# Layer 0's scale and shift dots of the second norm, placed beside the attention

## The chip, the cores and the metric

The kernel runs on one core of one Trainium2 chip. The metric is the device time of one execution, in microseconds (us). Engines are named as the profile names them: PE (TensorE) multiplies matrices, PEld loads its weights, DVE (VectorE) and ACT (ScalarE) work on whole tiles, POOL (GpSimd) and SP (SyncE) here issue transfers.

## The reference

Two layers of a decoder trunk on 512 tokens of width 1024, all in float32. Cut to what matters here:

```python
mod = (c_act @ w_ada + b_ada)[:, None, :]            # c_act = silu(c), one vector of 1024
sh1, sc1, g1, sh2, sc2, g2 = jnp.split(mod, 6, axis=-1)
h = rmsnorm(x, norm1_w) * (1 + sc1) + sh1
u = h @ w_in                                         # pool, conv, q, k, v, gate logits
...                                                  # pooling, short convolution, attention
merged = (gates[:, :, 0] * (y_pool @ p_pool)
          + gates[:, :, 1] * (y_conv @ p_conv)
          + gates[:, :, 2] * (y_attn @ p_attn))
x = x + g1 * (merged @ w_out)
h2 = rmsnorm(x, norm2_w) * (1 + sc2) + sh2
x = x + g2 * ((silu(h2 @ w_gate) * (h2 @ w_up)) @ w_down)
```

The modulation `mod` does not depend on `x`. Its six parts have 1024 numbers each; every one is a dot product of `c_act` with a column of `w_ada`.

## The kernel before, in words

**Matrix work.** Activations lie with features on the 128 partitions and the 512 tokens along the row, as eight tiles. Every product is made of three matmuls (`mm3`): both operands are split into a high and a low part, and high x high, high x low, low x high are summed. The low part of an activation is made on ACT and DVE (`split_from`, L671 to L680: a copy L675, a subtraction L676). Weights come in chunks of eight 128x128 blocks (512 KB) through a ring of three `raw` buffers; ACT writes the high part `whi`, DVE subtracts for `wlo` (`split_w`, L397 to L404). Chunks of the gate columns are split otherwise (`split_by_transfer`, L416 to L424): ACT writes `wlo` as minus the high part, and a transfer that POOL issues adds the weights from memory (L423). `next_w` keeps up to `ahead_now` chunks loaded ahead.

**The dots.** Of one part of `mod`, 128 numbers are one DVE instruction over a tile of 128x1024 (`ada_dot`, L477 to L480), so a part has eight dots. Each needs its own 512 KB load on SP's queue (L513). `ada_tasks` (L530) makes a list of tasks with a cost: 1.2 for a dot, 0.2 for a part's closing arithmetic. With `early` the loads go to the `raw` ring and stand one dot ahead; the first task is a load alone. Without it they go to the six spare tiles `w4`, which the attention uses too.

**What sets the order.** Side work stands in a list `bulk`. After every 2048 columns of `mm3`, that is, 12 full matmuls, there is a tick. It advances the running pieces of the attention (`fibers`) and then calls `run_bulk` with `bulk_rate`:

```python
credit[0] = min(credit[0] + amount, 4.0)
while bulk and credit[0] >= 0:
    cost, fn = bulk.popleft()
    credit[0] -= cost
    fn()
```

Credit goes on growing, up to 4, while the list is empty. `flush_bulk` runs what is left at once; `drain` ticks until no fiber is left. The framework's planner then orders each engine's instructions; those that are pinned (matmuls, weight splits on DVE, dots) keep program order among themselves on their engine.

**The stages around the change.** Once keys and values are there, three gates are computed, then convolution and pooling, then a fourth gate (`ready`). A loop over eight pairs `j` (L1212) then computes two gates each (two ticks a gate, those made ahead excepted) and the gated sum of pooling and convolution (one tick; L1209, L1226, into `m01`). The third gates and the attention's output follow in the order `GATE2`: six gates, attention steps 0 and 1, gates 6 and 7, attention steps 2 to 7. An attention step (L1244 to L1252) is 12 matmuls, the gated product L1209, the addition L1251 and the split into `merged[j]`. The attention itself runs in the ticks from before the fourth gate up to step 0, where `drain` ends it: scores, softmax on DVE and ACT (L796 to L817), transposes on PE (L161), products with the values. Behind it `tail` (L1261) makes the output projection, eight columns of 24 matmuls over `merged[0]` to `merged[7]`, adds it to `x` with `g1`, and prepares the second norm; the dots of G2 run beside it.

In layer 0, SC2's eight dots go through the `raw` ring beside the attention; the rate is 0 up to the third pair and 0.25 from there. G1's eight dots and, behind them, SH2's eight run at rate 1.5 from attention step 0 on. In layer 1 only G1 (rate 1.3) is left at that place, since SC2 and SH2 were made earlier; its list is empty beside the attention.

Of the kernel before, what the change touches and what calls it, by code (L numbers as in the profile page):

```python
# [63 lines left out]
SH1, SC1, G1, SH2, SC2, G2 = range(6)  # L64
# [19 lines left out]
def hybrid_trunk(ctx, tc, xT, ws, ada, cols, pool_w, qk_w, crow, pos, con, out):  # L84
# [22 lines left out]
    def ps_mm():  # L107
        return psum.tile([P, S], F32, tag="mm", name=nm("mm"), bufs=4)
# [16 lines left out]
    bulk = deque()  # L125
    bulk_rate, credit = [0.0], [0.0]
# [8 lines left out]
    def flush_bulk():  # L135
        while bulk:
            bulk.popleft()[1]()
# [12 lines left out]
    def drain():  # L150
        while fibers:
            tick()
# [10 lines left out]
    def mm3(o, lhs, rhs, start, stop, main=True, **more):  # L163
        matmul(o, lhs[0], rhs[0], start=start, stop=False, **more)
        matmul(o, lhs[0], rhs[1], start=False, stop=False, **more)
        matmul(o, lhs[1], rhs[0], start=False, stop=stop, **more)
        if main:
            clock[0] += o.shape[-1]
            if clock[0] >= TICK:
                clock[0] -= TICK  # L170
                tick()
# [105 lines left out]
    class GateUp:  # L277
# [9 lines left out]
        def load(self, sub):  # L287
            if sub < 2:
                return self.pair[sub].first()
            if sub < 6:  # L290
                return self.pair[sub % 2].sums(sub // 2 - 1)
            raw = rawt()
            fetch(raw, self.l, self.pair[0].blocks(1, 1) + self.pair[1].blocks(1, 1))
            return split_w(raw, C_BLOCKS)
# [159 lines left out]
    def next_w(ahead=None):  # L454
        ahead = ahead_now[0] if ahead is None else ahead
        while at[0] < len(items) and len(loaded) <= ahead:
            loaded.append(load_w())
        return loaded.popleft()

    def wblk(w, b):  # L460
        return w[0][:, b, :], w[1][:, b, :]
# [49 lines left out]
    def ada_load(l, part, j, early, kept):  # L511
        aw = wp.tile([P, D], F32, tag="raw", name=nm("raw"), bufs=RAW) if early else w4([P, D])
        nc.sync.dma_start(aw, ada[l, part, j])  # L513
        kept.append(aw)

    def ada_step(l, part, j, kept):
        aw = kept.pop(0)
        with tc.issue_after(dots_after[0].ins) if dots_after[0] is not None else nullcontext():
            ins = ada_dot(aw, l, part, j)
        pin(ins)  # L520

    def ada_end(l, part):
        m = mod[l][:, part]
        V.tensor_add(m, m, colt[:, l, C_ADA + part * KT:C_ADA + (part + 1) * KT])
        if part in (SC1, SC2):
            fold_scale(l, 0 if part == SC1 else 1, 0, KT)
        if part == G1:
            V.tensor_scalar(m, m, 0.5, None, op0=ALU.mult)

    def ada_tasks(l, parts, early=False):  # L530
        every = [(part, j) for part in parts for j in range(KT)]
        kept, out = [], []
        load = lambda n: ada_load(l, *every[n], early, kept)

        def step(n):
            if early and n + 1 < len(every):
                load(n + 1)
            if not early:
                load(n)
            ada_step(l, *every[n], kept)  # L540

        if early:
            out.append((1.2, lambda: load(0)))
        for n, (part, j) in enumerate(every):
            out.append((1.2, lambda n=n: step(n)))
            if j == KT - 1:
                out.append((0.2, lambda part=part: ada_end(l, part)))
        return out
# [122 lines left out]
    def split_from(src, scale=None):  # L671

        hi, lo = bigt(), bigt()
        if scale is None:
            A.activation(hi, src, AF.Copy)  # L675
            last_split[0] = V.tensor_sub(lo, src, f32(hi))  # L676
        else:
            A.activation(hi, src, AF.Copy, scale=scale)
            V.scalar_tensor_tensor(lo, src, scale, f32(hi), op0=ALU.mult, op1=ALU.subtract)
        return hi, lo  # L680
# [256 lines left out]
    for l in range(L):  # L937
# [238 lines left out]
        def gate():  # L1176
            g = ps_mm()
            feature_tile(g, next_w())
            sg = bigt(F32)
            A.activation(sg, g, AF.Tanh, scale=0.5)  # L1180
            return sg
# [17 lines left out]
            y_pool.append(split_from(pp, scale=col(C_PS + j)))  # L1199

        if l == 0:
            bulk.extend(ada_tasks(l, (SC2,), True))
        bulk_rate[0] = 0.0
        ahead_now[0] = 3
        ready.append(gate())
# [1 line left out]
        def gated(sg, branch):  # L1207

            V.scalar_tensor_tensor(sg, sg, 1.0, branch, op0=ALU.add, op1=ALU.mult)  # L1209

        pcw = None
        for j in range(KT):  # L1212
            s0, s1 = [ready.pop(0) if ready else gate() for _ in range(2)]
            if j == 2:
                bulk_rate[0] = 0.25
            if j % 2 == 0:
                pcw = next_w()
            b0 = 4 * (j % 2)
            p1, p2 = ps_mm(), ps_mm()
            for z in range(2):  # L1220
                mm3(p1, wblk(pcw, b0 + z), y_pool[z], z == 0, z == 1)
            for z in range(2):
                mm3(p2, wblk(pcw, b0 + 2 + z), y_conv[z], z == 0, z == 1)
            gated(s0, p1)
            gated(s1, p2)
            V.tensor_add(s0, s0, s1)  # L1226
            m01.append(s0)
# [4 lines left out]
        for step, j in GATE2:  # L1232
            if step == "gate":
                sg2[j] = gate()
                continue
            if j == 0:
                drain()
                flush_bulk()
                if l == 0:
                    bulk.extend(ada_tasks(l, (SH2,)))  # L1240
                late = len(bulk)
                bulk.extendleft(reversed(ada_tasks(l, (G1,))))
                bulk_rate[0] = 1.5 if l == 0 else 1.3
            if j % 2 == 0:  # L1244
                aw_ = next_w()
            p1 = ps_mm()
            for z in range(PAIRS):
                mm3(p1, wblk(aw_, 4 * (j % 2) + z), y_attn[z], z == 0, z == PAIRS - 1)
            t = sg2.pop(j)
            gated(t, p1)  # L1250
            V.tensor_add(t, t, m01[j])  # L1251
            merged.append(split_from(t))  # L1252
        while len(bulk) > late:
            bulk.popleft()[1]()


        def residual(k, src, lo, hi, part):
# [313 lines left out]
```

## Time and profile before

| | |
|---|---|
| median of 3 runs | 1446.27 us (1443.35 to 1450.1) |
| the profiled execution | 1442.51 us, span 1440.7 us |
| matmuls | 8298 in the span |
| PE / DVE / ACT / POOL busy | 99% / 74% / 52% / 12% of the span |
| mean granted PE clock | 0.999 |

The times of a view are in us from the span's first instruction. Matmuls are pipelined, so PE's busy share counts overlapping ends; what it loses is read from the distance of one matmul's start to the next. `L479` is a dot, with the spare tile `w` or the ring's `raw` as its operand.

### The profile page before, as it was taken

The page shows a single profiled execution, that of the slowest core. Times are in us where ns is not written, and L with a number is a line of the kernel's source. Part 1 is how long each engine was busy: PE and PEld are TensorE (multiplying, and loading weights), DVE is VectorE, ACT ScalarE, POOL GpSimd, SP SyncE. Part 2 cuts the span into 40 slices and gives each one's busy share as a digit, 9 for nine tenths or more (in the row PEclk, how much of TensorE's full clock was granted, in tenths as well). Part 3 has the DMA queues.
Part 4 walks back from the last instruction along what each step waited for, and adds up shares of the span by engine and source line. Part 5 has one row for each costly group of instructions (what it writes and reads, how often), then busy time and mean ns, then how long its engine had stood idle before and what let it go on. Part 6 is the DMA issues. An engine that isn't in the chain of part 4 may idle for free.

```text
span 1440.7 us, 22089 instructions
## 1 busy us (share of the span) xinstructions
PE 1428.3 (99%) x8298; PEld 1253.2 (87%) x8298; DVE 1062.3 (74%) x1944; ACT 750.8 (52%) x1260; POOL 165.7 (12%) x230
## 2 busy tenths in 40 slices
PE   9999999999999999999999999999999999999999
PEld 7887788887989998989988887888889989989997
DVE  8899767579786867767789986665878747657663
ACT  6776666633554452535454675666336525525450
POOL 0111000101100210211002000011020102111200
PEclk9999999999999999999999999999999999999999
DMA  9877666697446766747528665567773537646532
GB/s 359 234 199 192 175 162 161 159 322 236 119 128 213 196 177 203 191 131 209 195 88 248 170 149 133 133 158 186 253 207 84 141 109 180 172 109 184 138 85 85
DMA packets 94283, 251.28 MB, mean 174 GB/s; under 512 B 11992, under 2 KB 24672, under 8 KB 94176
## 3 DMA queue, kind: packets, MB, share of 16 engines
q1 hardware_dynamic: 67312, 177.37, 36.6%
q0 software_dynamic: 26272, 72.37, 25.3%
q8 instruction: 65, 1.06, 0.3%
q14 instruction: 42, 0.34, 0.1%
q10 hardware_dynamic: 592, 0.14, 0.0%
HBM read 247.73 MB, written 2.10 MB: 173 GB/s over the span
## 4 chain that ended last, share of the span: by engine, by line
PE 86%; DVE 8%; ACT 2%; DMA 2%; issue 1%; ACTq 0%; DVEq 0%; SPq 0%
PE mm L155 75%; PE pair L155 10%; DVE w L479 2%; DVE wlo L402 1%; PE mm L161 1%; DMA raw<-in_ws 1%; DMA wlo<-in_ws 0%; DVE big L676 0%; DMA w<-in_ada 0%; DVE big L1209 0%; DVE big L664 0%; DVE tmp L657 0%; ACT whi L419 0%; ACT big L675 0%; ACT whi L399 0%
## 5 line engine op out<-in xcount | busy, mean ns | idle before, releaser
L155 PE MATMUL mm<-big,whi 128*128 128x512 f32 (+1 forms) x4350 | 1080.4, 340 | 4.2 <-DVE big L676 1.9
L155 PEld LDWEIGHTS mm<-big,whi 128*128 128x128 f32 x4350 | 745.2, 190 | 92.9 <-DVE big L676 2.6
L155 PE MATMUL mm<-big,wlo 128*128 128x512 f32 (+1 forms) x2175 | 736.4, 339 | 0.4 <-DMA wlo<-in_ws 0.4
L155 PEld LDWEIGHTS mm<-big,wlo 128*128 128x128 f32 x2175 | 413.2, 190 | 46.3 <-issue 1.1
L399 ACT ACTIVATE whi<-raw 128x1024 fp32r<-128x1024 f32 (+2 forms) x186 | 191.6, 1031 | 194.1 <-PE mm L155 118.7
L402 DVE TENSOR_TENSOR wlo<-raw,whi 128x1024 fp32r<-128x1024 f32 (+2 forms) x186 | 218.8, 1185 | 41.6 <-ACT whi L399 40.9
L399 ACT ACTIVATE whi<-w 128x1024 fp32r<-128x1024 f32 x84 | 88.9, 1058 | 154.8 <-PE mm L155 94.7
L402 DVE TENSOR_TENSOR wlo<-w,whi 128x1024 fp32r<-128x1024 f32 x84 | 101.2, 1220 | 29.2 <-ACT whi L399 28.5
L1258 DVE SCALAR_TENSOR_TENSOR x<-mm,mod,x 128x512 f32<-128x512 f32 (+1 forms) x89 | 61.5, 693 | 74.1 <-PE mm L155 73.7
L479 DVE SCALAR_TENSOR_TENSOR w<-w,csil 128x1024 f32<-128x1024 f32 x88 | 105.0, 1219 | 13.0 <-DMA w<-in_ada 12.8
L261 POOL DMA_DIRECT2D w<-in_ws x72 | 47.9, 680 | 460.9 <-DVE wlo L402 258.6
L423 POOL DMA_DIRECT2D wlo<-in_ws x50 | 43.0, 861 | 388.1 <-ACT wlo L421 223.7
L263 POOL DMA_DIRECT2D w<-in_ws x72 | 63.9, 903 | 169.9 <-DMA w<-in_ws 162.8
L155 PE MATMUL pair<-whi,big 128*128 128x512 f32 x256 | 83.1, 390 | 0.0
L155 PE MATMUL pair<-big,whi 128*128 128x256 f32 (+1 forms) x376 | 74.0, 294 | 0.0
L419 ACT ACTIVATE whi<-raw 128x1024 fp32r<-128x1024 f32 x50 | 53.1, 1063 | 38.7 <-PE mm L155 28.5
L155 PEld LDWEIGHTS pair<-big,whi 128*128 128x128 f32 x376 | 60.4, 191 | 2.2
L155 PEld LDWEIGHTS pair<-whi,big 128*128 128x128 f32 x256 | 48.1, 188 | 9.9
L675 ACT ACTIVATE big<-big 128x512 fp32r<-128x512 f32 x52 | 32.5, 627 | 45.2 <-DVE big L1251 24.1
L155 PE MATMUL pair<-big,wlo 128*128 128x256 f32 (+1 forms) x188 | 55.4, 295 | 0.0
L421 ACT ACTIVATE wlo<-whi 128x1024 fp32r<-128x1024 f32 x50 | 52.6, 1059 | 0.4
L676 DVE TENSOR_TENSOR big<-tmp,big 128x512 fp32r<-128x512 f32 x48 | 33.0, 691 | 24.2 <-ACT big L675 23.2
(233 smaller groups left out, 1416.0 us busy)
## 6 DMA issues: line engine op xcount, KB each, us to landing
raw<-in_ws SPq DMA_DIRECT2D x146, 512.0 KB, 4.3
w<-in_ada SPq DMA_DIRECT2D x88, 512.0 KB, 5.8
w<-in_ws POOLq DMA_DIRECT2D x144, 256.0 KB, 4.6
wlo<-in_ws POOLq DMA_DIRECT2D x50, 512.0 KB, 6.5
raw<-in_ws SPq DMA_DIRECT2D x64, 256.0 KB, 3.8
raw<-in_ws SPq DMA_DIRECT2D x24, 384.0 KB, 3.3
raw<-in_ws SPq DMA_DIRECT2D x16, 448.0 KB, 6.4
raw<-in_ws SPq DMA_DIRECT2D x36, 128.0 KB, 3.2
```

Of the source, the lines that this page charges most:

```text
L155: tc.keep_in_program_order(T.matmul(*a, **k))
L261: nc.gpsimd.dma_start(dst, self.source(0, 1))
L263: nc.gpsimd.dma_start(dst, self.source(*other), accum_op=ALU.add)
L399: A.activation(hi[:, :n], raw[:, :n], AF.Copy)
L402: ins = V.tensor_sub(lo[:, :n], raw[:, :n], f32(hi)[:, :n])
L419: A.activation(hi[:, :n], raw[:, :n], AF.Copy)
L421: A.activation(lo[:, :n], f32(hi)[:, :n], AF.Copy, scale=-1.0)
L423: nc.gpsimd.dma_start(lo[:, i:i + m].rearrange("p b n -> p (b n)"), src, accum_op=ALU.add)
L479: return V.scalar_tensor_tensor(aw, aw, 1.0, csil, op0=ALU.mult, op1=ALU.mult, accum_out=mod[l][:, part, j:j + 1])
L675: A.activation(hi, src, AF.Copy)
L676: last_split[0] = V.tensor_sub(lo, src, f32(hi))
L1258: V.scalar_tensor_tensor(x[k][:, lo:hi], src, mod[l][:, part, k:k + 1], x[k][:, lo:hi], op0=ALU.mult, op1=ALU.add)
```

## The change

In layer 0, SH2's eight dots join SC2's in the list that goes through the `raw` ring beside the attention. The rate there is 0 up to the fourth pair (`j == 3`); from it on it is 0.45, counted from a credit of 0. From attention step 0 on, the list holds G1's eight dots alone, at rate 1.1 from a credit of 0; what is left of it behind step 7 is flushed. The last two points hold for layer 1 too, whose rate at that place was 1.3.

```diff
         if l == 0:
-            bulk.extend(ada_tasks(l, (SC2,), True))
+            bulk.extend(ada_tasks(l, (SC2, SH2), True))
         bulk_rate[0] = 0.0
...
-            if j == 2:
-                bulk_rate[0] = 0.25
+            if j == 3:
+                bulk_rate[0], credit[0] = 0.45, 0.0
...
             if j == 0:
                 drain()
                 flush_bulk()
-                if l == 0:
-                    bulk.extend(ada_tasks(l, (SH2,)))
-                late = len(bulk)
-                bulk.extendleft(reversed(ada_tasks(l, (G1,))))
-                bulk_rate[0] = 1.5 if l == 0 else 1.3
+                bulk.extend(ada_tasks(l, (G1,)))
+                bulk_rate[0], credit[0] = 1.1, 0.0
...
-        while len(bulk) > late:
-            bulk.popleft()[1]()
+        flush_bulk()
```

## The prediction

> **What bounds the kernel now.** I read the page first, then the chain of waits for layer 0's end of attention, then TensorE's instructions there in order of time, then the windows by stage.
>
> ```profile
> span 1440.7 us, 22089 instructions
> PE 1428.3 (99%) x8298; PEld 1253.2 (87%) x8298; DVE 1062.3 (74%) x1944; ACT 750.8 (52%) x1260; POOL 165.7 (12%) x230
> PE 86%; DVE 8%; ACT 2%; DMA 2%; issue 1%; ACTq 0%; DVEq 0%; SPq 0%
> ```
>
> TensorE (PE) sets the time: 86% of the chain. So an edit gains only where PE stands still, and loses only where it makes PE stand still. The 8% of DVE in the chain are the places to look at. Chain, 290 to 345 us:
>
> ```profile
> 290.03 15.98 PE mm L155 x74
> ...
> 321.04 5.76 DMA w<-in_ada
> ...
> 337.38 1.14 DVE w L479 x2
> 338.52 0.60 DVE big L676
> ...
> 339.84 0.64 ACT big L675
> ...
> 340.50 0.70 DVE big L676
> ```
>
> From 306 to 341 us the chain does not run through PE: it runs through VectorE's queue, with dots (L479) in it, to the splits L675/L676 of the last two merged tiles. The piece of "DMA" is a mislabel: VectorE was busy 16.86 of 17 us in that stretch (row 320:337 below), so it did not stand waiting for a load. What PE loses by it:
>
> ```profile
> 299.71 0.62 PE L155 MATMUL mm<-big,whi 128*128 128x512 f32 x2
> 300.17 0.39 PE L155 MATMUL mm<-big,wlo 128*128 128x512 f32 x1
> 300.39 0.61 PE L155 MATMUL mm<-big,whi 128*128 128x512 f32 x2
> ...
> 337.11 0.39 PE L155 MATMUL mm<-big,whi 128*128 128x512 f32 x1
> 339.18 0.50 PE L155 MATMUL mm<-big,whi 128*128 128x512 f32 x1 [1.68 <-DVE big L676]
> 339.51 0.40 PE L155 MATMUL mm<-big,wlo 128*128 128x512 f32 x1
> 340.52 0.50 PE L155 MATMUL mm<-big,whi 128*128 128x512 f32 x1 [0.61 <-ACT big L675]
> 341.25 0.79 PE L155 MATMUL mm<-big,whi 128*128 128x512 f32 x1 [0.23 <-DVE big L676]
> 341.84 0.63 PE L155 MATMUL mm<-big,wlo 128*128 128x512 f32 x1
> 342.26 1.05 PE L155 MATMUL mm<-big,whi 128*128 128x512 f32 x2
> 343.12 0.63 PE L155 MATMUL mm<-big,wlo 128*128 128x512 f32 x1
> 343.54 0.98 PE L155 MATMUL mm<-big,whi 128*128 128x512 f32 x2
> 344.36 0.39 PE L155 MATMUL mm<-big,wlo 128*128 128x512 f32 x1
> ```
>
> At its pace PE starts three matmuls in 0.68 us (299.71 to 300.39), 0.2267 each. From 337.11 to 344.36 it starts 11, worth 11 x 0.2267 = 2.49 us, in 7.25: **4.8 us lost**. Some 3.4 of it are waits on L676 and L675; the other 1.4 come behind them, where starts stand 0.43 apart (341.84, 342.26) and the granted clock is 0.51. By stage (span; PE, PEld, DVE, ACT, POOL busy; clock; DMA share; GB/s), layer 0 first, the last three rows the same stage of layer 1:
>
> ```profile
> 186.00:300.00 114.00, 114.00 (x595) 94.91 (x594) 73.10 (x206) 73.33 (x155) 12.06 (x14) 1.00 0.73 182
> 300.00:320.00 20.00, 20.00 (x90) 16.57 (x89) 18.83 (x32) 6.97 (x9) 0.00 (x0) 1.00 0.93 339
> 320.00:337.00 17.00, 17.00 (x77) 14.08 (x76) 16.86 (x27) 6.32 (x8) 0.00 (x0) 1.00 0.81 302
> 341.00:344.40 3.40, 3.17 (x9) 2.52 (x9) 3.40 (x4) 2.03 (x3) 0.00 (x0) 0.51 0.60 198
> 1011.00:1031.00 20.00, 20.00 (x90) 16.56 (x89) 17.50 (x28) 7.08 (x9) 0.00 (x0) 1.00 0.89 330
> 1031.00:1048.00 17.00, 17.00 (x76) 14.08 (x75) 13.64 (x19) 6.73 (x10) 0.00 (x0) 1.00 0.39 137
> 1048.00:1066.00 18.00, 18.00 (x81) 14.90 (x80) 17.22 (x27) 6.00 (x9) 4.86 (x7) 1.00 0.77 220
> ```
>
> Layer 1 is the model for layer 0 after the change: behind its attention stand only G1's and then G2's dots, and PE does not pause.
>
> **The change part by part.** Its dots, before (count, min/median/max ns, first and last start), layer 0 and then layer 1:
>
> ```profile
> L479 DVE SCALAR_TENSOR_TENSOR w<-w,csil x16: 1212/1218/1220, 299.6 to 337.3; 128x1024 f32<-128x1024 f32 x16
> L479 DVE SCALAR_TENSOR_TENSOR raw<-raw,csil x8: 1215/1217/1222, 147.3 to 251.8; 128x1024 f32<-128x1024 f32 x8
> L479 DVE SCALAR_TENSOR_TENSOR w<-w,csil x16: 1217/1220/1222, 1011.4 to 1064.0; 128x1024 f32<-128x1024 f32 x16
> ```
>
> *Taken out behind the attention:* SH2's eight dots, 8 x 1.22 = 9.8 us of VectorE, and their eight 512 KB loads. They stand in a stretch where VectorE has 35.69 busy us of 37 (18.83 + 16.86), so whatever leaves in front of the last merged tiles moves these up, until PE itself is their releaser. With PE at its pace, 337.11 is the 19th matmul of the first output column, which therefore begins at 337.11 - 18 x 0.2267 = 333.0; attention step 7 ends there. Its tile then needs L1209, L1251, L675, L676, some 0.65 to 0.7 each (L676 0.60, L675 0.64 in the chain): ready by 335.8. PE reads it at its 22nd matmul, 333.0 + 21 x 0.2267 = 337.8. The lead is 2.0 us; now the last split ends at 341.2 (340.50 + 0.70), 3.4 late. Moving it up by 3.4 needs three of the eight dots gone. **Gain: the whole 4.8 us**, the slow-clock part included, since it has no other cause in the rows.
>
> *G1 at 1.1 a tick from credit 0, not 1.5 from what was saved up.* The attention steps with gates 6 and 7 are 8 x 12 + 2 x 24 = 144 matmuls, 12 ticks. By the credit rule one dot runs in each of the first eight ticks and the end in the ninth, so the flush finds nothing, and three ticks stand free of dots ahead of the output projection. The credit kept there (0.1 + 3 x 1.1 = 3.4) lets four of G2's dots out at the projection's first tick; layer 1 does the same now (credit capped at 4) and its rows show PE at 18.00 of 18. Cost 0. In layer 1 the same edit spreads a burst over eight ticks in a stretch with PE at 20.00 of 20: 0, and no gain is possible there.
>
> *SC2's last five dots and SH2's eight beside the attention.* At 0.45 a tick from the fourth pair on: 13 x 1.2 + 0.4 = 16.0 of credit against 5 x 5 + 6 x 2 = 37 ticks x 0.45 = 16.65; the last dot falls in tick 33, so they fit. The first three dots still come at once, from the credit left over, as now. VectorE there is 73.10 of 114; eight more make 82.9, 73%, below layer 1's 17.50 of 20 at which PE does not wait. PE has 114.00 of 114, which excludes a gain. What excludes a loss, or not, is the lead of what PE reads:
>
> ```profile
> 225.34 0.48 DVE L817 TENSOR_SCALAR tmp<-tmp,asm 128x128 f32<-128x128 f32 x2
> ...
> 228.85 0.60 PE L161 MATMUL mm<-ident,tmp 128*128 128x128 f32 x4
> ```
>
> The scaled probabilities end at 225.8, and PE transposes them at 228.85: 3.0 us, the shortest such lead that I found in this stretch. Behind a dot on VectorE's in-order queue stand these softmax steps, the gated products that free PSUM banks, and L402's splits. A tick is 12 matmuls, 2.72 us, and the attention's own beside them; at one dot in 1.2 / 0.45 = 2.7 ticks, 7.3 us or more, one, at worst two, meet the same chain: 2.4 us against 3.0. Bounds: 0, and, if three hit each of ten remaining units, 10 x (3.66 - 3.0) = 6.6 us. I take 0, since the dots that stand there now, the last at 251.8, cost PE nothing.
>
> *Their loads:* eight of 512 KB move from the spare tiles to the ring of three raw buffers, which the weights use, and on SP's queue stand between the weights' fetches.
>
> ```profile
> SPq L239 <- DVE raw L479: 24.4, 3, 12.2
> ...
> 227.52 0.86 POOL L423 DMA_DIRECT2D wlo<-in_ws  x1 [17.83 <-DVE asm L803]
> DMA to landing us min/median/max: 5.4/7.1/9.4
> 252.12 0.58 ACT L1180 ACTIVATE big<-mm 128x512 f32<-128x512 f32 x1
> ```
>
> A fetch already waits up to 12.2 us for a dot to free its buffer. The weights survive it: the gate chunk whose last transfer was issued at 227.52, after a pause of 17.83, has landed by 236.9 at the longest landing; its gate (I count back from the last gate's transfer) is evacuated at 252.1, so began 24 x 0.2267 = 5.4 earlier, at 246.7, or somewhat before for attention work between: some 9 us of lead. A dot every 2.7 ticks holds its buffer for less than one every 1.2 / 0.25 = 4.8 ticks. Cost 0; the upper bound is rival C below. In bytes the stretch has 182 GB/s x 114 us = 20.7 MB; 4.2 more are a fifth, so its DMA share of 0.73 becomes about 0.88, under the 0.93 of 300:320 where PE did not wait.
>
> *Sum:* 4.8 gained, 0 lost. The profiled execution took 1442.51 us (span 1440.7 and 1.8 around it); it becomes 1437.7. The median of the runs shown is 3.8 higher, 1446.27: **1441.5 us**.
>
> **The rivals.** *Part of the stall stays (B).* The planner puts a dot of G2's burst or an L402 split (1.2 us) ahead of each of the three VectorE steps of the last tile: 3 x 1.2 - 2.0 = 1.6 us late. For: four dots come at the projection's first tick. Against: layer 1 has just that and no pause. Gain 4.8 - 1.6 = 3.2: 1443.1. The Trainium skill, "TensorE: Matmul & The Clock Gate", Part 1, says that the clock halves only after an idle window of about 3.4 us; the trace agrees as far as it goes (about 3.4 us of waits, then clock 0.51), and by that rule 1.6 us of waiting brings no slow clock; without the rule, in the present proportion, 0.7 would be added.
>
> *Slower (C): the ring of raw buffers.* If a weight's fetch stands behind a dot's buffer for the longest wait seen, 12.2 us, on top of the present pause, the 9 us of lead are overdrawn by 3.2; it decides as soon as the prefetch does not refill between two such waits. The present program has a dot-free stretch from 253 to 299 to refill; the new one has none. Three such events cost 9.6: net +4.8, 1451.1. Against it: half the hold time per dot. The Trainium skill, "Trainium Kernel Development and Optimization", Key Constraints, says that transfers issued from SP, ACT and POOL share the same 16 DMA engines and interleave, so the dots' loads would also lengthen L423's transfers; no row before shows by how much at this density.
>
> *It doesn't do what it says (D).* If ticks are fewer than 33, the rest of SH2 runs in the flush ahead of G1 and VectorE's backlog is as before: 1446.3. Against: the count of 37.
>
> *More (E).* PE also pauses once beside the attention:
>
> ```profile
> 157.33 0.39 PE L155 MATMUL mm<-big,wlo 128*128 128x512 f32 x1
> 159.22 0.55 PE L161 MATMUL mm<-ident,tmp 128*128 128x128 f32 x3 [1.50 <-DVE big L1209]
> ```
>
> 159.22 - 157.33 - 0.23 = 1.7 us, behind the burst of three dots at 147.3. The burst stays, but order and fetches around it are planned anew; without that pause 1439.8.
>
> **How the numbers follow.** Forecast 62%, B 15%, C 9%, D 5%, E 9%. The forecast's own spread, by the runs shown (1443.35 to 1450.1), is about 3.5 us to each side: 1438 to 1445. To hold 8 in 10 against sampling of the median and the other cases the range is 1436.5 to 1449; C's end is left out. The 0.5% that this kernel's measurement can tell is 7.2 us, so the gain of 4.8 (0.33%) lies inside: faster by more 14% (the low edge of the forecast, half of E), within 80%, slower by more 6% (C with more than three events).
>
> **What would show it.** Right: behind layer 0's attention eight dots of G1 and none of SH2; VectorE at 13 to 15 of 17 us in the second half; no PE pause at the first output column and no dip of the clock; 16 raw dots, from 147 to about 290, with PE full from 186 to 300. Wrong: PE idle before transposes (L161) or before a gate's matmuls, with L423 or a raw load as releaser; a remnant wait on L676; or a total more than 4.8 below, since the stretch holds no more.

## The result, and the profile after

The changed kernel takes 1453.07 us in the median (1447.88 to 1455.95), the kernel before, timed beside it, 1444.15 (1440.75 to 1450.1). The ratio, with its 95% interval in brackets, is **1.0058 [1.0048, 1.0068]**: slower by 8.9 us, where 4.8 us of gain were forecast. The time lies outside the range of 1436.5 to 1449, and on the side to which I had given 6%.

From the page of the changed kernel: span, busy times, shares of the chain of waits, and the group of the gate chunks' high parts (busy us, mean ns | idle time of ACT just before, and what ended it).

```profile
span 1450.7 us, 22082 instructions
PE 1429.7 (99%) x8298; PEld 1252.5 (86%) x8298; DVE 1062.0 (73%) x1944; ACT 750.7 (52%) x1260; POOL 165.5 (11%) x230
...
L419 ACT ACTIVATE whi<-raw 128x1024 fp32r<-128x1024 f32 x50 | 53.0, 1061 | 51.3 <-DMA raw<-in_ws 26.6
```

The same group before:

```profile
L419 ACT ACTIVATE whi<-raw 128x1024 fp32r<-128x1024 f32 x50 | 53.1, 1063 | 38.7 <-PE mm L155 28.5
```

The work is the same, as are PE's 8298 matmuls. New is that the high part of a gate chunk (L419) now waits mostly for the *load* of its raw tile, where before it mostly waited for PE.

To see where the time went I cut the span at three marks of the same program step: the first eight transposes (L161, x8) of the last unit of the second head pair, those of the fourth, and the second norm's statistic products. Between the first two lies nearly all the attention beside the gates, between the last two its end, the output projection and the norm. The windows of before (columns as in the prediction):

```profile
166.94:288.99 122.05, 122.05 (x646) 101.24 (x645) 81.23 (x228) 79.22 (x169) 12.92 (x15) 1.00 0.68 164
288.99:377.67 88.68, 86.17 (x409) 71.88 (x408) 71.10 (x116) 30.45 (x44) 8.62 (x12) 0.98 0.81 261
```

and after:

```profile
169.25:303.02 133.77, 125.01 (x646) 102.14 (x645) 87.88 (x240) 76.32 (x166) 12.06 (x14) 0.99 0.67 165
303.02:387.81 84.79, 84.61 (x408) 70.77 (x407) 64.56 (x104) 33.16 (x48) 10.38 (x14) 1.00 0.81 252
```

Behind the attention 88.68 - 84.79 = **3.9 us are gained**. Beside it, with the same 646 matmuls, 133.77 - 122.05 = **11.7 us are lost**: PE idles for 8.76 us, and its matmuls are busy 3.0 us longer (about 1.6 of it in one stretch at a low clock, last section; the rest I did not trace). Ahead of the first mark stand 169.25 - 166.94 = 2.3 us, though the program there is the same; behind the last, almost nothing (1063.0 us to the end of the span before, 1062.9 after). 2.3 + 11.7 - 3.9 - 0.1 = 10.0, the difference of the two spans. The dots came where they were meant to:

```profile
L479 DVE SCALAR_TENSOR_TENSOR raw<-raw,csil x16: 1215/1218/1224, 149.6 to 316.8; 128x1024 f32<-128x1024 f32 x16
L479 DVE SCALAR_TENSOR_TENSOR w<-w,csil x16: 1217/1218/1222, 319.2 to 368.0; 128x1024 f32<-128x1024 f32 x16
```

The largest pause, in the chain of waits after (start, duration, what):

```profile
195.38 1.15 DVE raw L479 x2
...
196.55 6.51 DMA raw<-in_ws
...
203.08 1.06 ACT whi L419
204.14 0.28 ACT tmp L843
...
204.44 0.42 DVE tmp L844
...
205.61 0.52 PE mm L161 x3
```

Read it from the top. A dot on VectorE ends and frees a raw buffer. Only now can SP issue the fetch of a gate chunk; it lands 6.5 us later. ACT then splits it, and only behind that does it make the attention's copy L843, through which PE's transposes are fed. ACT's instructions in order of time (in brackets its idle time before, and what ended it):

```profile
203.08 1.06 ACT L419 ACTIVATE whi<-raw 128x1024 fp32r<-128x1024 f32 x1 [3.42 <-DMA raw<-in_ws]
204.05 0.36 ACT L843 ACTIVATE tmp<-mm 64x256 f32<-64x256 f32 x1
...
286.32 1.06 ACT L419 ACTIVATE whi<-raw 128x1024 fp32r<-128x1024 f32 x1 [4.85 <-DMA raw<-in_ws]
287.28 0.58 ACT L828 ACTIVATE w<-mm 128x512 fp32r<-128x512 f32 x1
```

and PE's:

```profile
161.53 0.55 PE L161 MATMUL mm<-ident,tmp 128*128 128x128 f32 x3 [1.50 <-DVE big L1209]
...
199.80 0.28 PE L155 MATMUL mm<-w,big 128*128 128x256 f32 x1
...
202.68 0.49 PE L161 MATMUL mm<-ident,tmp 128*128 128x128 f32 x3
205.61 0.52 PE L161 MATMUL mm<-ident,tmp 128*128 128x128 f32 x3 [2.44 <-DVE tmp L846]
...
206.50 0.63 PE L155 MATMUL mm<-big,wlo 128*128 128x512 f32 x1
206.93 1.06 PE L155 MATMUL mm<-big,whi 128*128 128x512 f32 x2
...
288.64 0.74 PE L155 MATMUL mm<-w,big 128*128 128x256 f32 x4 [2.19 <-DVE w L829]
```

What L843 copies was ready when the product at 199.80 ended, at 200.1. L843 has nothing to do with the late chunk, yet it starts at 204.05: it stands behind L419 on ACT's in-order queue. The Trainium skill, "Perfetto Trace Analysis", Per-engine timelines, calls ACT, DVE and GpSimd strict FIFO; the trace agrees: ACT was idle for 3.42 us ahead of L419 and did not take L843 up. At 286 it is the same, with L828 behind L419. What PE then waits for, by the brackets, is the attention's L846 and L829, not the chunk. In the lists of waits between 165 and 310 us (total us, times, longest; the last two rows from SP's own list) this is

```profile
ACT whi L419 <- DMA raw<-in_ws: 19.5, 8, 4.9
...
PE mm L161 <- DVE tmp L846: 5.4, 4, 2.4
...
PE mm L155 <- DVE w L829: 3.4, 2, 2.2
...
SPq L513 <- DVE raw L479: 17.1, 4, 8.6
SPq L239 <- DVE raw L479: 12.8, 4, 5.8
```

The rows of before for ACT and for SP:

```profile
ACT whi L419 <- DMA raw<-in_ws: 3.0, 2, 2.0
```

```profile
SPq L239 <- DVE raw L479: 23.6, 2, 12.2
```

PE's two rows, six pauses, are all of its idle time between the first two marks, and none of them names a weight. Five of the six, 7.7 us together, stand behind a late L419 in ACT's order: 2.44 at 203, 1.16 at 242, 0.72 and 1.15 at 249 to 252, 2.19 at 286. The sixth, 1.04 at 295, follows the backlog that the one at 286 left, and a dot on VectorE lies in its chain too. SP's rows alone do not tell the kernels apart: before also waited for dots there, 23.6 us in two waits, while ACT waited 3.0. VectorE is busy 87.88 of 133.77 us, the DMA engines 0.67: neither is full.

### The profile page after: what moved, and what is told of

It reads as the page before. It is cut to its first block, busy times and chain, and to the rows that moved or that the text cites. A ratio compares the mean times of both kernels' runs of the same rounds, so it can differ in the third digit from the quotient of the medians.

```text
span 1450.7 us, 22082 instructions
## 1 busy us (share of the span) xinstructions
PE 1429.7 (99%) x8298; PEld 1252.5 (86%) x8298; DVE 1062.0 (73%) x1944; ACT 750.7 (52%) x1260; POOL 165.5 (11%) x230
## 4 chain that ended last, share of the span: by engine, by line
PE 83%; DVE 8%; ACT 4%; DMA 4%; issue 1%; SPq 0%; DVEq 0%; ACTq 0%
PE mm L155 71%; PE pair L155 11%; DMA raw<-in_ws 3%; DVE wlo L402 1%; PE mm L161 1%; DVE raw L479 1%; DVE w L479 1%; DVE big L1209 1%; ACT whi L419 1%; DMA wlo<-in_ws 0%; ACT tmp L790 0%; ACT whi L399 0%; ACT tmp L809 0%; ACT tmp L812 0%; ACT big L675 0%
## 5 line engine op out<-in xcount | busy, mean ns | idle before, releaser
L399 ACT ACTIVATE whi<-raw 128x1024 fp32r<-128x1024 f32 (+2 forms) x186 | 191.4, 1031 | 183.2 <-PE mm L155 95.7
L402 DVE TENSOR_TENSOR wlo<-raw,whi 128x1024 fp32r<-128x1024 f32 (+2 forms) x186 | 218.8, 1185 | 43.0 <-ACT whi L399 40.5
L399 ACT ACTIVATE whi<-w 128x1024 fp32r<-128x1024 f32 x84 | 88.9, 1058 | 153.4 <-PE mm L155 90.5
L402 DVE TENSOR_TENSOR wlo<-w,whi 128x1024 fp32r<-128x1024 f32 x84 | 101.2, 1221 | 29.6 <-ACT whi L399 28.9
L479 DVE SCALAR_TENSOR_TENSOR w<-w,csil 128x1024 f32<-128x1024 f32 x80 | 95.7, 1221 | 11.5 <-DMA w<-in_ada 11.4
L419 ACT ACTIVATE whi<-raw 128x1024 fp32r<-128x1024 f32 x50 | 53.0, 1061 | 51.3 <-DMA raw<-in_ws 26.6
```

The costliest lines, as they stand in the source:

```text
L399: A.activation(hi[:, :n], raw[:, :n], AF.Copy)
L402: ins = V.tensor_sub(lo[:, :n], raw[:, :n], f32(hi)[:, :n])
L419: A.activation(hi[:, :n], raw[:, :n], AF.Copy)
L479: return V.scalar_tensor_tensor(aw, aw, 1.0, csil, op0=ALU.mult, op1=ALU.mult, accum_out=mod[l][:, part, j:j + 1])
```

## The experiments

**The theory:** the pace of the dots in the shared raw ring delays the gate chunks' fetches; ACT waits for them, and the softmax queued behind on ACT starves PE. **The rivals:** VectorE's extra dots delay the softmax by themselves (V); or the weights come late for PE itself, rival C as I had priced it (W). All experiments change the kernel after, unless said otherwise. The table has the window between the first two marks (att) and between the last two (tail), taken as above, and the ratio to the kernel before in the same session; its last column is ACT's wait for raw weight tiles between 165 and 310 us, L419 and L399 together. Windows and waits come from one profiled execution of each kernel; that of pool_split was 2.9 us below its median, that of pool_split2 4.6 above.

| run | att | tail | ratio [95%] | ACT waits |
|---|---|---|---|---|
| before | 122.05 | 88.68 | | 3.0 |
| after | 133.77 | 84.79 | 1.0058 [1.0048, 1.0068] | 19.5 |
| spill | 121.69 | 85.25 | 0.9981 [0.9972, 0.9991] | 3.1 |
| rate_only | 127.20 | 87.28 | 1.0033 [1.0020, 1.0046] | 9.2 |
| split3 | 122.05 | 86.98 | 0.9993 [0.9982, 1.0003] | 8.7 |
| room | 136.26 | 85.48 | 1.0101 [1.0082, 1.0120] | 22.4 |
| no_load2 | 121.71 | 83.88 | 0.9965 [0.9952, 0.9977] | 0 |
| ring4b | 122.31 | 83.87 | 0.9977 [0.9967, 0.9987] | 7.1 |
| ring4b_before | 121.71 | 87.31 | 1.0003 [0.9993, 1.0013] | 0 |
| late_split | 124.26 | 87.03 | 1.0031 [1.0017, 1.0044] | 2.3 |
| pool_split | 124.67 | 84.50 | 1.0016 [1.0002, 1.0031] | 12.0 |
| pool_split2 | 127.76 | 88.47 | 1.0039 [1.0027, 1.0051] | 0 |
| whi4 | 122.18 | 86.75 | 1.0186 [1.0159, 1.0213] | 15.3 |

**The half behind the attention alone (spill).** The kernel before, with one line changed: what does not fit there runs on beside the projection.

```diff
-                bulk_rate[0] = 1.5 if l == 0 else 1.3
+                bulk_rate[0], credit[0] = 1.1, 0.0
```

> The kernel before with one line changed: behind the attention the list still holds G1's eight dots and then SH2's, but at rate 1.1 from a credit of 0 as in the change, so some five of SH2's dots run beside the output projection and none beside the attention. If the backlog on VectorE makes the pause at 337 us, three or more dots leaving take away 3.4 us of waits and the slow clock behind them: 4.8 us gained, ratio 0.997. If the pause has another cause (the transfers there, 0.8 to 0.9 of the DMA engines), it stays: 1.000.

The pace alone takes most of the stall at the tail, 88.68 - 85.25 = 3.4 us, and loses nothing beside the attention: 1440.45 us in the median, faster than both kernels of the case. So the gain did not need SH2's dots moved.

**A fourth raw buffer, first try (ring4, ring4_before, no_load).** Room for it was taken from the ring of high parts; no_load leaves out SC2's and SH2's loads and dots a standing tile of zeros instead.

```diff
-RAW, BIG = 3, 46
+RAW, BIG = 4, 46
...
-        hi = wp.tile([P, C_BLOCKS, P], F32R, tag="whi", name=nm("whi"), bufs=5)
+        hi = wp.tile([P, C_BLOCKS, P], F32R, tag="whi", name=nm("whi"), bufs=4)   # at all three places
...
```

> The changed kernel with four raw buffers in place of three (the high-part ring has four in place of five, for room). Theory (ring and ACT's queue): beside the attention, PE waits because splits of weight chunks (L419, L399) stand in ACT's in-order queue ahead of the softmax's copies and exponentials, and wait for a fetch that SP could not issue until a dot freed its raw buffer. With a fourth buffer these fetches go out earlier: PE's pauses between 186 and 305 us fall from some 11 us to under 3, and the time to about the kernel before or below (ratio 0.995 to 1.001). Rival (VectorE is too full): the dots still run at the same rate, the pauses stay, ratio about 1.006.

> Control for the run with four raw buffers: the kernel before with the same buffers. PE does not pause beside the attention there, so both theories expect the ratio 1.000 within 0.002; a deviation would be the price of the smaller high-part ring and is to be taken off the other run.

> The changed kernel with the 16 dots beside layer 0's attention made on one standing tile of zeros, without their loads: SC2 and SH2 of layer 0 are then their bias alone, so the product with the weights is left out. The dots stay where they are on VectorE at the same length. Ring theory: no buffer of the ring and no transfer is taken, PE's pauses beside the attention vanish (under 1 us from 186 to 305) and the time falls below the kernel before by the 4.8 us of the tail and perhaps the pause at 157 (1.7): ratio 0.995 to 0.997. VectorE theory: the pauses stay, ratio 1.004 to 1.007.

All three lose the pauses beside the attention (121.66, 121.71 and 121.71 us), but they take 1.0134 [1.0119, 1.0149], 1.0183 [1.0168, 1.0198] and 1.0167 [1.0152, 1.0182]: a high part less costs 21 to 27 us behind the second norm (from the last mark to the end 1084 to 1090 us, not 1063). Alone, the 121.7 looks like proof of the ring. It is none, as whi4 shows.

**The control for that (whi4):** three raw buffers as in after, four high parts.

> Control for the run with four raw buffers: the changed kernel with three raw buffers and the high-part ring cut from five to four. Ring theory: with three raw buffers the pauses beside layer 0's attention stay, some 8 to 13 us lost between 165 and 305 us, on top of what the smaller high-part ring costs elsewhere (1.018 in the other control): ratio about 1.02 to 1.027. If it was the smaller high-part ring that took the pauses away, there are none here either and the ratio is 1.013 to 1.016.

```profile
171.29:293.47 122.18, 122.01 (x647) 101.18 (x646) 87.30 (x240) 77.28 (x166) 13.09 (x15) 1.00 0.74 185
```

```profile
ACT whi L419 <- DMA raw<-in_ws: 9.0, 7, 3.6
...
ACT whi L399 <- DMA raw<-in_ws: 6.3, 2, 5.8
```

The expectation failed: without a fourth raw buffer PE does not pause either, though ACT still waits 15.3 us for raw tiles. Compared in order, ACT's splits stand later there, behind copies that in after they precede. The pair of the pause at 203, in whi4:

```profile
202.21 0.38 ACT L843 ACTIVATE tmp<-mm 64x256 f32<-64x256 f32 x1
...
205.32 1.06 ACT L419 ACTIVATE whi<-raw 128x1024 fp32r<-128x1024 f32 x1 [0.38 <-DMA raw<-in_ws]
```

That fits the theory's second half (a wait costs what stands behind it), but it takes the first three runs away as evidence on the ring.

**The clean set (room, ring4b, ring4b_before, no_load2).** Room now comes from one temporary and one `big` tile; room takes these away and adds nothing, ring4b adds the raw buffer, ring4b_before does that to the kernel before, and no_load2 is no_load with this room.

```diff
-RAW, BIG = 3, 46
+RAW, BIG = 3, 45          # ring4b, ring4b_before: 4, 45
...
-        return work.tile([P, S], F32, tag="tmp", name=nm("tmp"), bufs=5)
+        return work.tile([P, S], F32, tag="tmp", name=nm("tmp"), bufs=4)
...
+        if early:             # no_load2; still[0] is the standing tile
...
+            kept.append(still[0])
+            return
```

> Control: the changed kernel with four of the attention's work tiles (tmp) in place of five and 45 big tiles in place of 46, three raw buffers and five high-part buffers as in the change. It makes room for the next two. Expected by all theories: the pauses beside the attention stay (8 to 14 us from 165 to 310), plus a small price of the fewer work tiles; ratio 1.006 to 1.012. If the pauses go here too, they hang on the planner's order around any buffer count, not on the ring alone.

> As the control with four work tiles, with four raw buffers in place of three; the high-part ring has its five. If the number of raw buffers decides, PE loses under 2 us from 165 to 310 and the ratio is 4 to 9 us (0.003 to 0.006) below the control's. If the hold on the ring is not it, the loss is that of the control.

> Control for the run with four raw buffers and four work tiles: the kernel before with the same buffers. If the buffers alone make that run fast, this one is at 0.998 too. If it is the change that gains once the ring has room, this one keeps the tail's pause and is at 1.000 to 1.003.

> As the control with four work tiles, with the 16 dots beside layer 0's attention made on one standing tile of zeros, without loads (layer 0's SC2 and SH2 are then their bias alone; the product with the weights is left out). VectorE does the same dots. If the dots' hold on the ring is the source, PE loses under 2 us from 165 to 310. If the extra 1.22 us pieces on VectorE are, the loss is that of the control.

The windows of room, of ring4b and of no_load2, one fence each:

```profile
169.62:305.88 136.26, 126.54 (x646) 102.83 (x645) 87.94 (x240) 76.07 (x166) 12.06 (x14) 0.97 0.64 161
```

```profile
166.33:288.64 122.31, 122.05 (x646) 101.22 (x645) 88.01 (x240) 78.32 (x168) 12.93 (x15) 1.00 0.70 182
```

```profile
167.82:289.53 121.71, 121.71 (x646) 101.32 (x645) 87.93 (x240) 79.18 (x168) 12.94 (x15) 1.00 0.60 139
```

VectorE does the same in all three, 88 us in 240 instructions. Without the loads PE is never idle: **V has fallen** as the main cause: the same dots without loads cost nothing here. With the loads and one more buffer, 0.3 us is idle; with the loads and the old ring, 9.7. The transfers as such are no limit either, since ring4b moves at 182 GB/s what room moves at 161. So the loss needs the loads and the ring of three. How the fourth buffer helps is less clear: the planner orders each of these kernels anew, and whi4 shows that order alone can take the pauses away. ACT still waits 7.1 us in ring4b, and SP waits for dots 34.9 us there, more than the 29.9 of after, but for 6.0 at most and not 8.6. ring4b is 17.5 us below room, where 4 to 9 were expected; 14 of it lie beside the attention. The change on four buffers against the kernel before on four gains 0.26% (0.9977 against 1.0003), and ring4b, at 1439.63 us, beats both kernels. no_load2 leaves work out; its 1437.32 is no time of the kernel, and only says that without these loads the ratio is 0.9965.

**Pace or number (rate_only, split3).** rate_only is the kernel before, with the new pace for SC2's dots, which also starts a pair later and from a credit of 0, and no dot of SH2. split3 keeps the old pace, 0.25, and moves three of SH2's dots to the attention, five behind it, where the pace is the new one.

```diff
-            if j == 2:                                  # rate_only, on before
-                bulk_rate[0] = 0.25
+            if j == 3:
+                bulk_rate[0], credit[0] = 0.45, 0.0
...
-            bulk.extend(ada_tasks(l, (SC2,), True))     # split3, on before
+            bulk.extend(ada_tasks(l, (SC2, SH2), True, 0, KT + 3))
...
-                    bulk.extend(ada_tasks(l, (SH2,)))
+                    bulk.extend(ada_tasks(l, (SH2,), lo=3))
...
-                bulk_rate[0] = 1.5 if l == 0 else 1.3
+                bulk_rate[0], credit[0] = 1.1, 0.0
```

> The kernel before with only the pace beside layer 0's attention changed: SC2's dots wait for the fourth pair and then run at 0.45 a tick from a credit of 0; SH2 stays behind the attention at the old rate. If it is the pace at which dots and weight fetches take turns in the ring that makes PE wait, the changed kernel's pauses up to SC2's last dot (about 237 us) come back: some 4.1 us at 203 to 209 and 3.6 at 241 to 252, none at 286 and 295, and the tail's 4.8 us stay: ratio 1.004 to 1.006. If it is the number of dots (16 through the ring), nothing is lost: 1.000.

> A version meant to beat both. The kernel before, with the old pace beside the attention (0.25 a tick from the third pair) but three of SH2's dots added to the list there, and behind the attention G1's eight dots and SH2's other five at 1.1 a tick from a credit of 0. If the pace and not the number hurts, the attention stays without pauses up to 300 us and the tail's pause goes altogether: ratio 0.996 to 0.998, at or below the run at rate 1.1 alone (0.9981). If more dots through the ring hurt at any pace, PE pauses between 252 and 300 and the ratio is 1.000 or above.

The windows of rate_only and of split3:

```profile
167.29:294.49 127.20, 123.09 (x646) 100.90 (x645) 81.23 (x228) 78.98 (x169) 12.92 (x15) 1.00 0.65 157
```

```profile
169.50:291.55 122.05, 122.02 (x647) 101.26 (x646) 83.43 (x232) 77.62 (x167) 12.06 (x14) 1.00 0.68 167
```

rate_only has before's eight dots (VectorE 81.23 us, x228, to the digit) and loses 5.2 us, at a ratio slightly below the expected one; split3 has three more dots at the old pace and loses nothing. In these two plans the new pace, with its later start, costs, and three dots more do not. ACT waits about as long in both (9.2 and 8.7 us), so the pace does not act through the sum of these waits. split3 still did not gain as expected, because at the tail two tiles stay late:

```profile
340.79 0.50 PE L155 MATMUL mm<-big,whi 128*128 128x512 f32 x1 [0.96 <-ACT big L675]
341.51 0.50 PE L155 MATMUL mm<-big,whi 128*128 128x512 f32 x1 [0.22 <-DVE big L676]
342.82 0.49 PE L155 MATMUL mm<-big,whi 128*128 128x512 f32 x1 [0.58 <-ACT big L675]
343.55 0.50 PE L155 MATMUL mm<-big,whi 128*128 128x512 f32 x1 [0.23 <-DVE big L676]
```

**ACT's queue itself (late_split, pool_split, pool_split2).** Ring, dots and fetches stay; only who makes the gate chunks' splits, or when, changes. late_split queues the split on ACT behind the tanh of the gate during which the chunk is fetched, pool_split gives it to POOL, pool_split2 gives POOL the other splits of that stretch (L399, L402) too.

```diff
-        A.activation(hi[:, :n], raw[:, :n], AF.Copy)    # late_split; after: the gate's tanh
+        with tc.issue_after(after.ins) if after is not None else nullcontext():
+            A.activation(hi[:, :n], raw[:, :n], AF.Copy)
...
-        A.activation(hi[:, :n], raw[:, :n], AF.Copy)    # pool_split
+        if on_pool:
+            nc.gpsimd.tensor_copy(hi[:, :n], raw[:, :n])
...
-        A.activation(lo[:, :n], f32(hi)[:, :n], AF.Copy, scale=-1.0)
+        if on_pool:
+            nc.gpsimd.tensor_scalar(lo[:, :n], f32(hi)[:, :n], -1.0, None, op0=ALU.mult)
...
```

> The changed kernel with one difference beside layer 0's attention: the high-part copy L419 of a gate chunk is queued on ACT behind the tanh of the gate during which the chunk is fetched, in place of wherever the planner put it (it puts it as early as it believes the fetch to have landed). Dots, ring, fetches and buffers stay. Theory (ACT's order around a late fetch makes the pauses): PE's loss from 165 to 310 us falls from 11.9 to under 4 and the tail's gain is left: ratio 0.997 to 1.001. If the ring's hold itself is what PE feels, through late weights, the pauses stay: 1.005 or more.

> The changed kernel with the two ACT copies of the gate chunks (L419, L421) made on POOL from the fourth gate to the last gate ahead of the attention's output, in layer 0 alone. The ring, the dots and the fetches stay as in the change, so the fetches still wait for dots. If the step from a late fetch to PE's pause is ACT's in-order queue, the softmax no longer stands behind a split and PE's pauses beside the attention fall from 11.9 us to a few (what is left would be chunks that are late themselves, since POOL's copies are slower): ratio 0.998 to 1.002. If the weights themselves are late for PE, the pauses stay or grow: 1.006 or more.

> The changed kernel with every split of a weight chunk beside layer 0's attention made on POOL: those of the gate chunks, as in the run before, and both parts of the chunks for pooling and convolution (L399 and L402 off ACT and VectorE). The pauses left in that run at 235 to 245 and at 285 came behind an L399 that waited for its fetch on ACT. If ACT's in-order queue is the whole step, they go (under 1.5 us lost from 165 to 305) and the gain at the tail is left: ratio 0.996 to 0.999. If the chunks are late for PE or POOL cannot keep up, PE waits for L423 or for POOL and the ratio is 1.001 or more.

The window and the waits for raw tiles of late_split,

```profile
167.20:291.46 124.26, 122.61 (x646) 101.22 (x645) 86.58 (x238) 79.41 (x170) 13.79 (x16) 1.00 0.74 185
```

```profile
ACT whi L399 <- DMA raw<-in_ws: 2.3, 2, 2.0
```

and of pool_split:

```profile
168.41:293.08 124.67, 122.82 (x646) 100.99 (x645) 96.21 (x240) 50.11 (x138) 66.36 (x42) 1.00 0.70 176
```

```profile
POOL whi L421 <- DMA raw<-in_ws: 42.1, 8, 13.3
ACT whi L399 <- DMA raw<-in_ws: 12.0, 3, 5.0
```

**W has fallen.** In pool_split the splits wait for late chunks for 42.1 us, up to 13.3 at once, twice what ACT waited, and PE idles for 1.85 us instead of 8.76: the chunks have the lead for it there. One pause of late_split, 0.6 us at 309.60, behind the attention, does wait for a weight (the transfer that completes `wlo`). The loss beside the attention drops from 11.7 to 2.6, with late_split to 2.2, though neither touches the ring. So most of what stops PE is what stands behind the wait on ACT. The totals are not as good: late_split was expected at the kernel before or below and is 0.3% above it. Its profile has 2.2 us beside the attention, 1.7 gained at the tail, and 2.1 more behind the second norm, whose origin I did not trace. In pool_split2, which was to bring the loss to nothing, it is 5.7. POOL is busy there for 78 of 127.76 us, and L402's low parts come from it too; this run brought waits of its own and decides nothing.

## Why the prediction was wrong

**The gain: right for this profile, the slow-clock part in part by luck.** "The whole 4.8 us": runs in which nothing else is late (ring4b, no_load2) show the tail at 83.87 and 83.88, 4.8 below 88.68. The change itself got 3.9 of it. It leaves 0.2 us of idle time; the other 0.7 lies in matmuls that were busy longer, which I did not trace. But 1.4 of the 4.8 was the slow clock behind the pause, and rate_only, whose program at the tail is that of before, has the same pauses without it:

```profile
344.69 0.50 PE L155 MATMUL mm<-big,whi 128*128 128x512 f32 x1 [1.68 <-DVE big L676]
346.03 0.50 PE L155 MATMUL mm<-big,whi 128*128 128x512 f32 x1 [0.61 <-ACT big L675]
346.76 0.50 PE L155 MATMUL mm<-big,whi 128*128 128x512 f32 x1 [0.22 <-DVE big L676]
```

Its granted clock from 341 to 350 us is 1.00, and its tail takes 87.28 us, 1.4 less than before's. "No other cause in the rows" was thus too strong: the stall itself is worth 3.4 us, the dip only where it comes. After the change the clock is 1.00 from 342 to 360 us; VectorE is busy for 23.78 of the 32 us up to 342 and for 17.68 of the 18 from there, and PE idles for 0.2.

**"G1 at 1.1 a tick": right.** The burst of G2's dots that follows, five in a row and not four, costs nothing; rival B did not come true. D did not either: eight dots of G1 and eight of G2 stand behind the attention, none of SH2, and the last raw dots come one by one, without a burst, so the count of ticks held; the last stands at 316.8, not at about 290, in part because of the pauses (in no_load2 at 299.0). E's pause stayed: 1.50 us of idle time ahead of L161, now at 161.53.

**"SC2's last five dots and SH2's eight beside the attention", VectorE's share: right.** The leads before L161 sufficed, as no_load2 shows.

**"Their loads: cost 0": this step failed.** I looked up how much lead a chunk has before *PE* reads it, found some 9 us, and concluded that a late fetch is survived. But the chunk's first reader is ACT, and ACT's queue is in order; there the copy waits at the time at which it was planned, far ahead of need, with the softmax behind it. Lead at the last reader says nothing of that. Among the signs that I had named as wrong was PE idle before L161 with a raw load as releaser; it came, with the load further up: raw tile, L419, L843, L844, L846, L161. The row was in the trace of before: L419 already waited 3.0 us for raw tiles, twice, and I did not read it. Nor was the sentence "holds its buffer for less" the right measure. From the issue of its load to its end a dot holds a buffer for 28 to 33 us before (the fifth to the eighth dot) and 10 to 25 after (the sixth to the sixteenth): shorter, as I said. But the dots follow each other more closely, so together they hold 1.6 of the three buffers before, from 173 to 253 us, and none behind that; after, it is 1.8 from 194 to 318 us.

**Rival C named the place, not the mechanism.** The ring was right, and so was "the new one has no dot-free stretch". Its price came from overdrawn lead, 3 x 3.2 = 9.6 us, near the 11.7 measured; but PE did not wait for weights (W fell with pool_split), so that nearness is chance. Its condition, overdrawn lead, was too strict: ACT's waits were 4.9 us at most, well within 9, and cost all the same. That is why 9% was too little.

**The sum by what was measured:** -3.9 + 11.7 = +7.8 in the profile, against 8.9 between the medians. The 2.3 us ahead of the first mark are in the profile too; whether they belong to the change stays open, since the program there is the same and the first mark of the other runs lies anywhere from 165.7 to 173.1.

**Open as well:** how much ACT waits does not set the loss by itself (split3 8.7 us and no loss, rate_only 9.2 and 5.2, whi4 15.3 and none). Which instructions stand behind does; that was followed pause by pause in after alone, and in the other runs rests on the moved splits. Why the planner put the splits where it did, and so whether the loss would come back under another order, was not examined.

## What to carry to other kernels

When a transfer may come later, ask for its *first* reader and for everything queued behind that reader on an in-order engine, not for the lead of the last reader. For work that goes through a ring shared with the weights, look at its pace and not only at its amount: in these runs eight dots cost nothing at one in 4.8 ticks and 5 us at one in 2.7, and sixteen at one in 2.7 cost next to nothing with one more buffer. A run that frees room for such a buffer needs its own control, because taking the room can move the effect by itself.

## What the runs showed of the hardware that was not expected

Three windows of the changed kernel around pauses of PE:

```profile
200.00:210.00 10.00, 7.56 (x30) 5.95 (x29) 4.30 (x14) 6.89 (x16) 0.86 (x1) 0.83 0.65 161
250.00:254.00 4.00, 2.76 (x14) 2.05 (x14) 2.53 (x9) 3.97 (x14) 0.00 (x0) 1.00 0.83 134
286.00:294.00 8.00, 5.81 (x28) 4.60 (x28) 5.91 (x18) 6.22 (x13) 0.86 (x1) 1.00 0.44 95
```

After 2.44 us of idle time at 203 the matmuls start 0.43 us apart (206.50, 206.93) and the granted clock is 0.83 of the window; after 2.19 us at 286 it is 1.00. The Trainium skill, "TensorE: Matmul & The Clock Gate", Part 1, puts the halving behind an idle window of about 3.4 us; here 2.44 us were enough once, so in the prediction that page's rule was too kind a measure for short pauses. The prediction's own rows did not agree with it as well as it says: their brackets add up to 1.68 + 0.61 + 0.23 = 2.52 us, not 3.4, ahead of the clock of 0.51. Nor does the length decide: rate_only has 1.68 + 0.61 + 0.22 and stays at 1.00. Counted without the six transposes, PE makes no product for 3.05 us at 203 (202.83 to 205.88) and slows down, and for 2.96 at 249 (249.32 to 252.28) and does not. What decides between these cases is not shown. The slow stretch cost about 1.6 us: from 205.88 to 209.49 nine matmuls start, worth 9 x 0.2267 = 2.0 us at full pace, in 3.6.
